# Head over seven gate/up pairs, two products for three, and gemvs moved to TensorE in a two-block transformer kernel

## The chip, the cores and the metric

The kernel runs on one core of one Trainium2 chip. The metric is the device time of one execution in microseconds. The engines are named as in the profile: PE is TensorE (PEld its weight loads), DVE VectorE, ACT ScalarE, POOL GpSimd, SP the engine that issues most DMAs.

## The reference, cut

Two blocks run on x of 256 rows and 1024 channels. The first has two layers; each is an FFN, a mixer (a pooling mixer, then attention) and a second FFN, and each of the three is modulated by vectors that come from c:

```python
mods = jnp.split(c_silu @ ada_w[layer] + ada_b[layer], N_MOD, axis=-1)
sh, sc, g = mods[0], mods[1], mods[2]
h = modulate(rms_norm(x, norm_g[layer, 0]), sh, sc)
x = x + 0.5 * (1.0 + g)[:, None, :] * swiglu(h, ffn_w_in[layer, 0], ffn_w_out[layer, 0])
```

`swiglu(h, w_in, w_out)` is `(silu(h @ w_g) * (h @ w_u)) @ w_out` with 2816 inner channels. The pooling mixer subtracts h from its mean over 2, 4, 8 or 16 rows, in four groups of channels, multiplies each group by a matrix, and scales. After the first layer keys and values are projected. The second block has a state-space branch and a latent attention, gated and merged. All is float32.

## The kernel before

x lies transposed as `X`: 128 channels on the partitions, eight slices kb, 256 rows of x in the free dimension. Every float32 weight tile of 512 KB (`wraw`, eight blocks of 128x128) is split into two float32r tiles: ACT casts it to the high part `whi` (L225), DVE subtracts to get the low part `wlo` (L216). The activations are split in the same way into `hhi` and `hlo`, in the FFN's inner layer into `shi` and `slo`. One block of a matrix product is then three products on PE, high by high, low by high, high by low (`mm3`, L350 to L352), each of 256 columns, into one PSUM bank. `mm3b` (L356 to L358) does the same with the roles exchanged and 512 columns.

The class `Stream` hands out weight tiles. Its `next()` splits tiles ahead of their use, up to four, and issues DMAs of later ones, with five raw buffers and five split ones. `Kernel.next` flushes functions that were put off (`defer`) by so many calls, and runs work from a list in the background by a budget. That list holds gemvs: `gemv(j)` takes a 512 KB tile of modulation weights (`graw`, three buffers) and the broadcast vector `cb` and writes 128 modulation values into column j of `modc`, in one DVE instruction (L377). A few gemvs run on PE instead, three at each seam between stages (`GAPS`, `gemv_pe`, L396), on tiles that were laid out for it. `ADA_SEQ` is the order of all gemv tiles in memory and on the DMA queue.

The order of all instructions is that of the code. Each engine works off its own queue in order, and so does SP with its DMAs; semaphores join them.

The FFN (`ffn`, L549) multiplies the input by pairs of gate and up tiles, 22 pairs; `act` applies silu on ACT (L558), multiplies on DVE (L560), copies the high part on ACT (L562) and subtracts on DVE (L563). The output tiles, eight of 22 blocks each, are added to X by `update` (L545), and ACT squares each new slice for the next norm (`st_add`), whose sums POOL adds up (L470) and PE reduces (`st_sum`, L486). `st_reduce` raises the sum to the power -1/2 on POOL (L506), `st_spread` turns it into a row by a transpose (L512). At a seam the parts of a PE gemv (`self.gap`) are issued between these steps.

The first FFN begins differently, since its modulation isn't there yet. This is the head: `ffn` works with four pairs at once (`lead`), slice by slice, and before slice k calls `feed(k)`, which takes the two gemvs of this slice (shift and scale, on DVE), modulates slice k of X (`mod_a`, L519 on DVE and L520 on ACT; `mod_b`, L524 on DVE) and splits one weight tile. PE then does the 4 x 2 x 3 products of the slice. The first norm's squares are added up by DVE and POOL.

In the pool stage (`pool_mixer`, L619) PE multiplies the modulated input by the group matrices; the result `pz` is multiplied by constant pooling matrices `pm`, an output tile at a time (L646, L647), and `update` follows.

## Time and profile before

| | us |
|---|---|
| median of three runs | 1333.29 (1330.23 to 1335.79) |
| the profiled execution | 1332.45 |
| its span, first to last instruction | 1330.6 |
| PE busy | 1274.8, 96% of the span, 10378 instructions |
| PE weight loads busy | 1210.3, 91% |
| DVE busy | 1008.7, 76%, 1751 instructions |
| ACT busy | 668.9, 50% |
| POOL busy | 163.9, 12% |
| DMA | 331.21 MB, mean 249 GB/s |

PE is busy nearly all the time, but its instructions overlap: one product is on record for 0.28 us, and the next starts 0.12 us after it. Its busy time therefore says that something was in it, not that it ran at its best, and spacings are what to read. The engines' shares are averages over stages that differ; the windows in the section of rows take the stages apart.

### The profile page before, as it was taken

The page shows a single profiled execution, that of the slowest core. Times are in us where ns is not written, and L with a number is a line of the kernel's source. Part 1 is how long each engine was busy: PE and PEld are TensorE (multiplying, and loading weights), DVE is VectorE, ACT ScalarE, POOL GpSimd, SP SyncE. Part 2 cuts the span into 40 slices and gives each one's busy share as a digit, 9 for nine tenths or more (in the row PEclk, how much of TensorE's full clock was granted, in tenths as well). Part 3 has the DMA queues.
Part 4 walks back from the last instruction along what each step waited for, and adds up shares of the span by engine and source line. Part 5 has one row for each costly group of instructions (what it writes and reads, how often), then busy time and mean ns, then how long its engine had stood idle before and what let it go on. Part 6 is the DMA issues. An engine that isn't in the chain of part 4 may idle for free.

```text
span 1330.6 us, 26407 instructions
## 1 busy us (share of the span) xinstructions
PE 1274.8 (96%) x10378; PEld 1210.3 (91%) x10378; DVE 1008.7 (76%) x1751; ACT 668.9 (50%) x1162; POOL 163.9 (12%) x282
## 2 busy tenths in 40 slices
PE   5899999999999999999998999999999999999998
PEld 4899999899999779999997989999988888988996
DVE  6898887698998789988977687878754576346774
ACT  3454434555444555444436554444365765236542
POOL 1000011100001100020111101000100791110000
PEclk9999999899999999999998999999999999989999
DMA  8999998487899578988974368877765533786752
GB/s 299 333 340 338 325 335 306 140 329 255 270 311 337 214 268 273 306 307 305 341 287 164 127 225 259 275 242 276 258 224 171 167 104 112 185 212 198 279 182 79
DMA packets 122287, 331.21 MB, mean 249 GB/s; under 512 B 27633, under 2 KB 42865, under 8 KB 122098
## 3 DMA queue, kind: packets, MB, share of 16 engines
q1 hardware_dynamic: 122018, 328.73, 72.9%
q8 instruction: 81, 1.33, 0.4%
q0 software_dynamic: 144, 0.79, 0.2%
q14 instruction: 44, 0.36, 0.1%
HBM read 317.94 MB, written 10.49 MB: 247 GB/s over the span
## 4 chain that ended last, share of the span: by engine, by line
PE 54%; ACT 4%; DVE 3%; DMA 3%; issue 1%; SPq 1%; POOL 0%; DVEq 0%; ACTq 0%; POOLq 0%
PE psA L350 5%; PE psA L352 4%; PE psB L352 4%; PE psB L350 4%; PE psB L351 4%; PE psA L351 4%; PE psD L350 3%; PE psD L352 3%; PE psD L351 3%; PE psC L350 2%; PE psC L352 2%; PE psC L351 2%; PE psA L356 1%; DMA wraw<-in_w 1%; PE psA L357 1%
## 5 line engine op out<-in xcount | busy, mean ns | idle before, releaser
L216 DVE TENSOR_TENSOR wlo<-wraw,whi 128x1024 fp32r<-128x1024 f32 x391 | 478.8, 1230 | 46.6 <-ACT whi L225 45.9
L225 ACT CAST whi<-wraw 128x1024 fp32r<-128x1024 f32 x391 | 403.4, 1047 | 120.3 <-ACT whi L225 46.9
L377 DVE SCALAR_TENSOR_TENSOR junk<-graw,cb 128x1024 bf16<-128x1024 f32 x166 | 203.9, 1228 | 24.6 <-DMA graw<-in_ada 21.0
L350 PE MATMUL psD<-hhi,whi 128*128 128x256 f32 x560 | 160.3, 286 | 0.4 <-ACT hhi L520 0.4
L352 PE MATMUL psD<-hlo,whi 128*128 128x256 f32 x560 | 159.1, 284 | 0.0
L351 PE MATMUL psD<-hhi,wlo 128*128 128x256 f32 x560 | 159.1, 284 | 0.0
L350 PE MATMUL psA<-hhi,whi 128*128 128x256 f32 x480 | 138.6, 289 | 5.0 <-ACT whi L225 3.3
L351 PE MATMUL psA<-hhi,wlo 128*128 128x256 f32 x480 | 137.3, 286 | 5.9 <-DVE wlo L216 5.9
L350 PE MATMUL psB<-hhi,whi 128*128 128x256 f32 x488 | 138.9, 285 | 0.0
L352 PE MATMUL psB<-hlo,whi 128*128 128x256 f32 x488 | 138.6, 284 | 0.0
L351 PE MATMUL psB<-hhi,wlo 128*128 128x256 f32 x488 | 138.6, 284 | 0.0
L352 PE MATMUL psA<-hlo,whi 128*128 128x256 f32 x480 | 136.7, 285 | 0.0
L350 PEld LDWEIGHTS psD<-hhi,whi 128*128 128x128 f32 x560 | 108.1, 193 | 2.1 <-issue 1.4
L352 PEld LDWEIGHTS psD<-hlo,whi 128*128 128x128 f32 x560 | 108.1, 193 | 0.2 <-DVE hlo L524 0.2
L351 PEld LDWEIGHTS psD<-hhi,wlo 128*128 128x128 f32 x560 | 108.1, 193 | 0.0
L350 PEld LDWEIGHTS psA<-hhi,whi 128*128 128x128 f32 x480 | 92.5, 193 | 8.8 <-ACT whi L225 4.5
L351 PEld LDWEIGHTS psA<-hhi,wlo 128*128 128x128 f32 x480 | 92.7, 193 | 7.3 <-DVE wlo L216 7.3
L350 PE MATMUL psA<-shi,whi 128*128 128x256 f32 x352 | 99.2, 282 | 0.0
L352 PE MATMUL psA<-slo,whi 128*128 128x256 f32 x352 | 98.6, 280 | 0.0
L350 PE MATMUL psB<-shi,whi 128*128 128x256 f32 x352 | 98.5, 280 | 0.0
L352 PE MATMUL psB<-slo,whi 128*128 128x256 f32 x352 | 98.5, 280 | 0.0
L351 PE MATMUL psB<-shi,wlo 128*128 128x256 f32 x352 | 98.1, 279 | 0.0
(453 smaller groups left out, 3201.4 us busy)
## 6 DMA issues: line engine op xcount, KB each, us to landing
graw<-in_ada SPq DMA_DIRECT2D x184, 512.0 KB
wraw<-in_win SPq DMA_DIRECT2D x176, 512.0 KB
wraw<-in_w SPq DMA_DIRECT2D x93, 512.0 KB
wraw<-in_wout SPq DMA_DIRECT2D x88, 512.0 KB
wraw<-in_wkv SPq DMA_DIRECT2D x16, 512.0 KB
Hd<-ct SPq DMA_DIRECT2D x16, 256.0 KB
Gd<-gsb SPq DMA_DIRECT2D x16, 256.0 KB
wraw<-in_wq SPq DMA_DIRECT2D x8, 512.0 KB
```

The lines of the kernel that those rows point to most:

```text
L216: self.nc.vector.tensor_sub(lo, raw, hi.bitcast(F32))
L225: self.nc.scalar.copy(hi, raw)
L350: mm(out, hi[:, b], ah, start=first, stop=False)
L351: mm(out, lo[:, b], ah, start=False, stop=False)
L352: mm(out, hi[:, b], al, start=False, stop=last)
L356: mm(out, ah, whi, start=first, stop=False)
L357: mm(out, ah, wlo, start=False, stop=False)
L377: self.nc.vector.scalar_tensor_tensor(junk, self.gemv_tile(j), 1.0, self.cb, op0=OP.mult, op1=OP.mult, accum_out=self.modc[:, j:j + 1])
```

## The change

It has three parts.

**The head.** `LEAD` is 7: seven pairs are computed slice by slice, in seven banks that hold gate and up side by side. The squares of X are no longer added up: each of the eight slices is reduced by PE, all into one PSUM tile. Eleven of the modulation tiles get buffers of their own (`headp`). The gemvs of six shift tiles (2, 4, 6, 8, 10, 12) run on PE, two in the middle of slices 0, 2 and 4 (`hooks` 7), and their results are transposed and added to the shift at the slice's end (`hooks` 14). The activations of pairs 0 to 5 are called within the last slice.

**Two products for three.** High and low part of an activation lie side by side in one tile (`hhl`, `shl`, `ohl`). In seven of eight output tiles of each FFN and of the attention's output projection, `mm2` multiplies the high weight by both parts at once, 512 columns, and the low weight by the high part, 256 columns. The bank then holds two sums, and `update` adds both to X.

**Gemvs in the pool stage.** The gap of the first FFN now holds tiles 54 to 56; tiles 57 to 63 are loaded into buffers of the pool stage and worked off on PE in two groups, ahead of its output tiles 0 and 4.

```diff
-HEAD_LAG = 1
+LEAD = 7
-    return 4 if (l, f) == (0, 0) else 2
+    return LEAD if (l, f) == (0, 0) else 2
-GAPS = {"g00": (61, 62, 63), "gpool": (64, 65, 66), "g01": (104, 105, 106), "g10": (128, 129, 130),
+GAPS = {"g00": (54, 55, 56), "gpool": (64, 65, 66), "g01": (104, 105, 106), "g10": (128, 129, 130),
-HEAD_PE = ()
+HEAD_PE = {0: (2, 4), 2: (6, 8), 4: (10, 12)}
+POOL_PE = ((57, 58, 59, 60), (61, 62, 63))
...
+    def mm2(self, out, hi, lo, b, a, first, last):
+        mm = self.nc.tensor.matmul
+        mm(out, hi[:, b], a.rearrange("p x t -> p (x t)"), start=first, stop=False)
+        mm(out[:, :T], lo[:, b], a[:, 0], start=False, stop=last)
...
     def update(self, kb, ps, g, eng=None, late=None):
-        self.nc.vector.scalar_tensor_tensor(self.X[:, kb], ps, g[:, kb:kb + 1], self.X[:, kb],
-                                            op0=OP.mult, op1=OP.add)
+        for i in range(0, ps.shape[1], T):
+            self.nc.vector.scalar_tensor_tensor(self.X[:, kb], ps[:, i:i + T], g[:, kb:kb + 1], self.X[:, kb],
+                                                op0=OP.mult, op1=OP.add)
...
+    def lead_pass(self, pp, hh, k, b, hooks):
+        for i, p in enumerate(pp):
+            for x in range(2):
+                if b % 8 == 0:
+                    self.lead_w = self.next()
+                hi, lo = self.lead_w
+                self.mm3(p[:, x * T:(x + 1) * T], hi, lo, b % 8, hh[:, k], k == 0 and x == 0, k == 7, True)
+                b += 1
+                if 2 * i + x + 1 in hooks:
+                    hooks[2 * i + x + 1]()
+        return b
...
+                pp = [self.ps(t) for t in "ABDDABC"]
...
+                self.lead_pass(pp, hh, KB - 1, b, {2 * i + 2: (lambda i=i: act(i - 1, pp[i - 1][:, :T], pp[i - 1][:, T:]))
+                                                   for i in range(1, n0)})
+                self.defer(act, n0 - 1, pp[-1][:, :T], pp[-1][:, T:])
...
-                    self.mm3(p[:, :T], hi, lo, b % 8, shi[:, k], slo[:, k], k == 0, k == FB - 1)
-                self.defer(self.update, n, p[:, :T], g)
+                    mm(p[:, :w], hi, lo, b % 8, ss[:, k], k == 0, k == FB - 1)
+                self.defer(self.update, n, p[:, :w], g)
...
+            for r in POOL_PE:
+                ts = [pp.tile([128, D], F32, name="pg%d" % j) for j in r]
+                for j, t in zip(r, ts):
+                    nc.sync.dma_start(t, self.h["ada"][ADA_POS[j]])
...
+                if n in (0, 4):
+                    side = self.gemv_pe(*gs[n // 4])
+                    side[0](0, KB)
+                    side[1](False)
+                elif n in (2, 6):
+                    side[2]()
...
+            for half in range(2):
+                for kb in (0, 2, 1, 3):
+                    kb += 4 * half
+                    sq = self.KT[:, kb]
+                    if kb % 4 < 2:
+                        nc.scalar.activation(sq, self.X[:, kb], AF.Square)
+                    else:
+                        V.tensor_mul(sq, self.X[:, kb], self.X[:, kb])
+                    if kb < 7:
+                        self.st_sum(sq, kb == 0, False)
...
+            self.st_reduce()
+            hgemv(1)
+            hgemv(0)
...
             def feed(k):
...
+                self.ws.split((14 * k + 21) // 8, los)
...
+                hr = self.mod_a(rbs, g0, h0, k)
+                los.pop(0)()
+                self.mod_b(hr, g0, h0, k)
+                while los:
+                    los.pop(0)()
+                js, n = more[k]
+                hdma(*js)
+                self.ws.dma(n)
                 if k + 1 < KB:
+                    hgemv(2 * k + 3)
...
+                def mm():
+                    pe[0](0, KB)
+                    pe[1](False)
+
+                def fin():
+                    nc.tensor.transpose(hps[:, 256:384], self.grow, self.ident)
+                    V.tensor_add(g0[:, 1, k + 1:k + 3], hps[:, 256:320:32], self.adab[:, js[0]:js[0] + 3:2])
+                    self.done.update(js)
+                return {7: mm, 14: fin}
```

How it moves instructions shows in the engines' queues; each row is line, operation, what it writes and reads, size, and the semaphores that it waits for by their engine. On DVE in the head, from one slice to the next, before (`junk` is a gemv, `hraw` and `hlo` are the modulation and the input's low part):

```order
L377 SCALAR_TENSOR_TENSOR junk,modc<-graw,cb 128x1024 [waits DMAHW5_49,DVE_49]
L998 SCALAR_TENSOR_TENSOR gain<-modc,gate 128x1
L1001 TENSOR_TENSOR gain<-modc,adab 128x1
L519 SCALAR_TENSOR_TENSOR hraw<-X,gain,rbs 128x256 [waits DVE_49]
L377 SCALAR_TENSOR_TENSOR junk,modc<-graw,cb 128x1024 [waits DMAHW6_49]
L524 SCALAR_TENSOR_TENSOR hlo<-hraw,gain,hhi 128x256 [waits Activation_49]
L216 TENSOR_TENSOR wlo<-wraw,whi 128x1024 [waits DMAHW4_49,Activation_49]
```

and after, from slice 0 to slice 1:

```order
L220 TENSOR_TENSOR wlo<-wraw,whi 128x1024 [waits DMAHW2_49]
L991 SCALAR_TENSOR_TENSOR junk,modc<-hg_149,cb 128x1024 [waits DMAHW5_49]
L1086 TENSOR_TENSOR gain<-psC,adab 128x2 [waits PE_49]
L1054 SCALAR_TENSOR_TENSOR gain<-modc,gate 128x1 [waits DVE_49]
L530 SCALAR_TENSOR_TENSOR hraw<-X,gain,rbs 128x256 [waits DVE_49]
L220 TENSOR_TENSOR wlo<-wraw,whi 128x1024 [waits DMAHW6_49,Activation_49]
L535 SCALAR_TENSOR_TENSOR hhl<-hraw,gain,hhl 128x256 [waits Activation_49]
```

One of two gemvs is gone, the low weight part stands ahead of the input's low part, and ahead of the modulation stands an add that waits for PE.

On ACT at the end of the head, from the last modulated slice on, before:

```order
L520 ACTIVATE hhi<-hraw,gain 128x256 [waits DVE_49]
L225 CAST whi<-wraw 128x1024 [waits DMAHW6_49,PE_49,Activation_49]
L225 CAST whi<-wraw 128x1024 [waits DMAHW0_49,PE_49,Activation_49]
L225 CAST whi<-wraw 128x1024 [waits DMAHW2_49,PE_49,Activation_49]
L225 CAST whi<-wraw 128x1024 [waits DMAHW3_49,PE_49,Activation_49]
L558 ACTIVATE sg<-psA 128x256 [waits PE_49]
L562 CAST shi<-sf 128x256 [waits DVE_49]
L225 CAST whi<-wraw 128x1024 [waits DMAHW4_49,Activation_49]
```

and after, the last of six activations and what follows it:

```order
L588 ACTIVATE sg<-psA 128x256 [waits PE_49,Activation_49]
L592 CAST shl<-sf 128x256 [waits DVE_49]
L588 ACTIVATE sg<-psB 128x256 [waits PE_49,Activation_49]
L592 CAST shl<-sf 128x256 [waits DVE_49]
L229 CAST whi<-wraw 128x1024 [waits DMAHW5_49]
L229 CAST whi<-wraw 128x1024 [waits DMAHW6_49]
```

Four more such pairs of a silu and a copy stand ahead of these, directly behind the modulated slice; no weight cast is among them.

On SP, from the end of the first FFN into the pool stage, before (`graw_2713` and the rows like it are gemv tiles in the three shared buffers):

```order
L211 DMA wraw_2681<-in_win01 128x1024 [waits DMAHW7_49,DMAHW0_49,DVE_49]
L363 DMA graw_2713<-in_ada 128x1024 [waits PE_49]
L363 DMA graw_2715<-in_ada 128x1024 [waits DMAHW1_49,PE_49]
L211 DMA wraw_2749<-in_win01 128x1024 [waits DMAHW3_49,DMAHW2_49,DVE_49]
L211 DMA wraw_2870<-in_win01 128x1024 [waits DMAHW4_49,DVE_49]
L363 DMA graw_2929<-in_ada 128x1024 [waits PE_49]
```

and after:

```order
L372 DMA graw_2575<-in_ada 128x1024 [waits PE_49]
L372 DMA graw_2577<-in_ada 128x1024 [waits DMAHW2_49,PE_49]
L215 DMA wraw_2611<-in_win01 128x1024 [waits DMAHW4_49,DMAHW3_49,DVE_49]
L661 DMA pg57_2663<-in_ada 128x1024
L661 DMA pg58_2664<-in_ada 128x1024 [waits DMAHW5_49]
L661 DMA pg59_2665<-in_ada 128x1024 [waits DMAHW6_49]
L661 DMA pg60_2666<-in_ada 128x1024 [waits DMAHW7_49]
L661 DMA pg61_2671<-in_ada 128x1024 [waits DMAHW0_49]
L661 DMA pg62_2672<-in_ada 128x1024 [waits DMAHW1_49]
L661 DMA pg63_2673<-in_ada 128x1024 [waits DMAHW2_49]
L215 DMA wraw_2745<-in_win01 128x1024 [waits DMAHW3_49,DVE_49]
L372 DMA graw_2873<-in_ada 128x1024 [waits DMAHW4_49,PE_49]
```

The seven loads of the pool stage stand behind two loads into shared buffers that wait for PE, and ahead of the tiles of the pool stage's own gap.

## Rows read from the trace of the kernel before

**Rows 1.** Windows: busy us (x instructions) of each engine, clock, DMA share, GB/s.

```profile
18.77:55.42 36.65, 29.66 (x192) 27.18 (x192) 31.99 (x63) 13.45 (x18) 0.00 (x0) 0.95 0.91 320
55.42:72.90 17.48, 17.48 (x145) 17.44 (x145) 16.83 (x28) 10.59 (x19) 0.00 (x0) 1.00 0.88 311
72.90:221.58 148.68, 148.68 (x1250) 148.55 (x1248) 125.20 (x178) 65.26 (x89) 7.86 (x7) 1.00 0.94 339
...
165.00:221.00 56.00, 56.00 (x478) 56.00 (x477) 44.94 (x58) 20.82 (x25) 7.86 (x7) 1.00 0.93 347
```

**Rows 2.** Timeline of PE, products of 512 columns: start us, us, what.

```profile
1301.32 0.40 PE L356 MATMUL psA<-whi,mh 128*128 128x512 f32 x1
...
1305.86 0.39 PE L358 MATMUL psB<-whi,ml 128*128 128x512 f32 x1
```

**Rows 3.** Timeline of PE in the head, with the idle time before an instruction.

```profile
11.80 1.01 PE L486 MATMUL psC<-ones,stacc 128*128 128x1 f32 x4 [5.79 <-POOL stacc L470]
12.67 0.99 PE L486 MATMUL psC<-ones,stlast 128*128 128x1 f32 x4
...
20.62 0.41 PE L350 MATMUL psB<-hhi,whi 128*128 128x256 f32 x1
20.84 0.41 PE L351 MATMUL psB<-hhi,wlo 128*128 128x256 f32 x1
...
34.81 0.58 PE L351 MATMUL psA<-hhi,wlo 128*128 128x256 f32 x1 [2.05 <-DVE wlo L216]
```

**Rows 4.** Timeline of ACT, start and end of the head.

```profile
5.00 0.42 ACT L459 ACTIVATE stacc<-X 128x256 f32<-128x256 f32 x1 [2.77 <-DMA X<-in_xT]
...
54.99 0.38 ACT L558 ACTIVATE sg<-psA 128x256 f32<-128x256 f32 x1
55.86 0.41 ACT L562 CAST shi<-sf 128x256 fp32r<-128x256 f32 x1 [0.49 <-DVE sf L560]
56.17 1.99 ACT L225 CAST whi<-wraw 128x1024 fp32r<-128x1024 f32 x2
```

**Rows 5.** Timeline of DVE, one slice of the head.

```profile
19.89 1.22 DVE L377 SCALAR_TENSOR_TENSOR junk<-graw,cb 128x1024 bf16<-128x1024 f32 x1
...
21.03 0.22 DVE L998 SCALAR_TENSOR_TENSOR gain<-modc,gate 128x1 f32<-128x1 f32 x1
...
21.28 0.48 DVE L519 SCALAR_TENSOR_TENSOR hraw<-X,gain,rbs 128x256 f32<-128x256 f32 x1
...
22.83 0.48 DVE L524 SCALAR_TENSOR_TENSOR hlo<-hraw,gain,hhi 128x256 fp32r<-128x256 f32 x1
23.28 1.23 DVE L216 TENSOR_TENSOR wlo<-wraw,whi 128x1024 fp32r<-128x1024 f32 x1
```

**Rows 6.** Timeline of PE, from the first FFN's end through the pool stage.

```profile
221.58 0.61 PE L396 MATMUL psC<-graw,cc 128*1 128x128 f32 x12
...
223.22 0.83 PE L396 MATMUL psC<-graw,cc 128*1 128x128 f32 x18
...
225.86 0.39 PE L356 MATMUL psA<-whi,hhi 128*128 128x256 f32 x1 [0.36 <-ACT hhi L520]
...
233.52 0.59 PE L646 MATMUL psA<-pm,pz 128*128 128x256 f32 x2
234.17 0.60 PE L646 MATMUL psB<-pm,pz 128*128 128x256 f32 x2
...
247.62 0.58 PE L350 MATMUL psA<-hhi,whi 128*128 128x256 f32 x1
```

**Rows 7.** Windows, with the granted clock (third from the end).

```profile
227.00:232.00 5.00, 4.67 (x34) 4.13 (x34) 4.68 (x11) 3.59 (x9) 0.00 (x0) 1.00 0.98 388
34.70:38.00 3.30, 3.19 (x15) 3.20 (x16) 3.30 (x9) 1.42 (x2) 0.00 (x0) 0.50 0.92 286
242.90:249.60 6.70, 6.13 (x52) 4.26 (x52) 4.31 (x9) 2.05 (x6) 1.62 (x1) 0.50 0.10 16
```

**Rows 8.** Timeline of SP's queue at the seam.

```profile
225.52 0.81 SPq L363 DMA_DIRECT2D graw<-in_ada  x2
```

More of the change, by code (lines that the diff above doesn't have):

```diff
@@ L80 @@
     ADA_SEQ += [j for j in range(a0, a1) if j not in ON_PE] + list(GAPS.get(gap, ()))
+    if gap == "g00":
+        ADA_SEQ += [j for r in POOL_PE for j in r]
 ADA_POS = {j: i for i, j in enumerate(ADA_SEQ)}
@@ L241, in next @@
         self.nh += 1
-        if self.nh >= 6 and self.ahead < HLB - 1:
+        if self.ramp and self.ahead < HLB - 1:
             self.ahead += 1
-            self.depth = RAWB
         return r
@@ L345, in flush, with mm3, mm @@
             f(*a)
-    def mm3(self, out, hi, lo, b, ah, al, first, last):
+    def mm3(self, out, hi, lo, b, a, first, last, shared=False):
+        def mm(*a, **kw):
+            self.nc.tensor.matmul(*a, skip_group_check=shared, **kw)
+        mm(out, hi[:, b], a[:, 0], start=first, stop=False)
+        mm(out, lo[:, b], a[:, 0], start=False, stop=False)
+        mm(out, hi[:, b], a[:, 1], start=False, stop=last)
+    def mm2(self, out, hi, lo, b, a, first, last):
         mm = self.nc.tensor.matmul
-        mm(out, hi[:, b], ah, start=first, stop=False)
-        mm(out, lo[:, b], ah, start=False, stop=False)
-        mm(out, hi[:, b], al, start=False, stop=last)
+        mm(out, hi[:, b], a.rearrange("p x t -> p (x t)"), start=first, stop=False)
+        mm(out[:, :T], lo[:, b], a[:, 0], start=False, stop=last)
     def mm3b(self, out, ah, al, whi, wlo, first, last):
@@ L604, in ffn, with proj_a @@
             self.st_half(D, gap)
-    def proj_a(self, ah, al, evac, kb=KB, tiles=8, tags="AB", T_=T, late=True):
+    def proj_a(self, a, evac, kb=KB, tiles=8, tags="AB", late=True, wide=0):
         hi = lo = None
@@ L934, in phase1, with hdma, hgemv @@
             ssm = self.ssm_items()
[L935 to L960 removed]
+            hs = ExitStack()
+            headp = hs.enter_context(self.tc.tile_pool(name="headp", bufs=1))
+            order = [2, 4, 3, 5, 6, 8, 7, 9, 10, 12, 11]
+            def hdma(*js):
+                for j in js:
+                    if j in order:
+                        t = headp.tile([128, D], F32, name="hg%d" % j)
+                    else:
+                        t = self.gpool.tile([128, D], F32, name="graw")
+                    nc.sync.dma_start(t, h["ada"][j])
+                    self.graw[j] = t
+            def hgemv(j):
+                junk = self.jpool.tile([128, D], BF, name="junk")
+                nc.vector.scalar_tensor_tensor(junk, self.graw.pop(j), 1.0, self.cb, op0=OP.mult, op1=OP.mult,
+                                               accum_out=self.modc[:, j:j + 1])
+                self.done.add(j)
+                self.slot()
+            hdma(1, 0)
+            self.cols = load("cols", [128, 100])
+            self.adab = load("adab", [128, NADA])
+            self.ws.dma(2)
+            hdma(2, 4, 3)
+            self.ws.dma(4)
+            hdma(5)
+            self.ws.dma(5)
             nc.scalar.activation(self.halfpi, self.ones, AF.Silu)
@@ L992, in phase1 @@
             V.tensor_mul(hg[:, 1], hg[:, 1], hg[:, 0])
+            more = [((6, 8, 7), 7), ((9,), 9), ((10, 12, 11), 11), ((13,), 12), ((14, 15), 14), ((), 16),
+                    ((), 18), ((), 19)]
             def feed(k):
@@ L1617, in zs_step @@
                     gelu(n - 6)
-            self.proj_a(hh, hl, zs_step, tags="CD", late=True)
+            self.proj_a(hh, zs_step, tags="CD", late=True)
             def gs_evac(n, p):
```

298 lines of the change are left out of this document (136 added, 162 removed).

## The prediction, made before the change was run

> **What bounds the kernel now.** I read the page's slices first, then windows by stage, then the queues at the places that the change touches. The windows [rows 1] show three kinds of stretch. From 72.90 to 221.58 us, the rest of the first FFN, PE is busy for all 148.68 us, one product every 0.12 us; the other three FFNs look the same. There only fewer or cheaper products help. From 18.77 to 55.42, the head, PE issues 192 products in 36.65 us, where 192 x 0.12 = 23 would do: it waits for DVE, which is busy for 31.99 us. The third kind is the seams between stages, of which the pool stage is one (221.6 to 247.6). So an edit is worth what it does to PE's products, to the head, and to that seam; DVE work removed from 72.90 to 221.58 is worth nothing.
>
> The profiled execution took 1332.45 us, with a span of 1330.6; the median of the three runs is 1333.29. The sum is made against 1332.45 and the difference of 0.8 is left within the range.
>
> **Edit 1: two products instead of three (output matmuls of the FFNs, 7 of 8 tiles, and 7 of 8 of the attention's).** It concerns 4 x 7 x 22 + 7 x 8 = 672 triples. Now each is three products of 256 columns; 478 of them stand in 56.00 us [rows 1], 0.118 us each with the edge rows off, 354 ns a triple. After, it is one of 512 and one of 256 columns. Products of 512 columns stand in the last stage: 20 spacings between 1301.32 and 1305.86, 227 ns each [rows 2]. So a pair costs 227 + 118 = 345, and 9 ns a triple are saved: what goes is the fixed part of one product, 2 x 120 - 227 = 13 ns at most. 672 x 9 = 6.3 us off PE's path; bounds 7 and 14 ns, so 4.5 to 9.5. The price is a second X update on DVE for 35 tiles, 0.39 us each. From 165 to 221 us, in the first output stage, DVE is busy for 44.9 of 56 us [rows 1], and 7 x 0.39 = 2.7 fits into the idle 11; without that cover all 35 would cost 14 us. I cost it at nothing.
>
> A page of the Trainium skill speaks against this edit: "TensorE: Matmul & The Clock Gate", section "Wait — 56ns, not 53.3ns?", gives a fixed cost of about 2.5 ns per matmul beside its columns. By it, as an estimate, 672 x 2.5 = 1.7 us would be saved. The spacings of 120 and 227 ns in this trace do not agree with it, and the sum goes by them.
>
> **Edit 2: the head.** Before, the 336th product ends at 72.9 us: 192 by 55.42 and 144 more in 17.48 [rows 1]. Those are 14 weight tiles' worth. After, the same 336 are seven pairs over eight slices, 42 products a slice. I work out when PE has done them.
>
> Start. The 16 sums of squares (two per slice of X) cost PE 0.87 us per slice at the early rate, from 11.80 to 12.67 [rows 3]. X is there at 5.0 [rows 4], so they end between 9 (at the full rate) and 12.4; I take 11.4. In DVE's new order the sums' result stands ahead of both first gemvs, so behind it come two gemvs of 1.14, gains, a modulation, a weight remainder of 1.14 and 0.45 for the input's remainder [rows 5], some 5 us, and further waits of about 1 us for ACT, whose two casts (1 us each) now stand ahead of the modulated input. PE starts in effect at 17.5 (16 to 18.5); before, its fourth product starts at 20.62 [rows 3], in effect 20.3.
>
> Products: 336 x 0.12 = 40.3. The first products before follow each other every 0.21 us [rows 3], and so for about 4.5 us; after such a start again, 2.6 us lost (1.7 to 3.4).
>
> Three gemv pairs in PE's queue, in the middle of slices 0, 2 and 4: three k-steps take 0.83 us [rows 6], whose last 0.27 overlap, so eight take 1.75; with the change of form 1.9 each, 5.7 together (5.2 to 6.6).
>
> **The new wait.** Behind slices 0, 2 and 4 PE transposes the gemv's row, DVE adds it to the shift, and only then come the gain and the modulation of the next slice, since DVE works in order. Queued behind that add are modulation, weight remainder and input remainder, for which PE waits. From [rows 4, 5]: transpose 0.3, add 0.15, gain 0.2, modulation 0.4 (start to start), weight remainder 1.14, input remainder 0.48. That is 2.7 until PE's third product; 0.24 of it is covered by two products that need no remainder. So 2.45 each, 7.4 for three (5 to 8). The odd slices need no such add: there DVE has 4.6 us of work from one input remainder to the next, PE 5.04, so DVE is hidden (0.2 for slice 7).
>
> The end of the head. Before, one activation stood ahead of each weight cast. Now ACT has six in a row, and each is silu, wait for DVE's product, copy: from 54.99 to 56.17 that takes 1.18 us [rows 4], while PE delivers a pair every 0.72. The first can start 36 products before PE's last, less 0.2 of latency, so 4.1 us. 6 x 1.18 = 7.1, so the next weight cast starts 2.9 us after it, takes 1.05, and its remainder 1.23: PE goes on 5.2 us late (3 to 6). Such waits have a second price: before product 34.81 PE was idle for 2.05 us [rows 3], and from 34.7 to 38.0 the granted clock was 0.50; from 242.9 to 249.6 it was so again [rows 7]. I add 2.0 for the one here (0 to 3.4) and 1.5 for the three smaller waits together (0 to 5).
>
> Sum: 17.5 + 40.3 + 2.6 + 5.7 + 7.4 + 0.2 + 5.2 + 3.5 = 82.4, against 72.9: **9.5 us slower**. All low ends together give 71.2, so -1.7; all high ends +18.8. I keep +2 to +16. DMA does not decide: the head needs 34 tiles of 512 KB, and the queue gave 388 GB/s [rows 7], 1.35 us a tile, so the last lands by 50 us, 15 ahead of its use. The gemvs' own buffers thus buy nothing beyond what PE can use.
>
> **Edit 3: seven gemvs from DVE to PE in the pool stage.** Off DVE go 7 x 1.22 = 8.5 us in a stretch where PE never waits: 0. On PE come two groups of 1.9, and a transfer: the seven tiles are loaded in the pool stage. SP comes to them at about 226, because two loads into the three shared buffers stand ahead (of tiles 57 and 58 a second time, which nothing reads) and wait until PE has read the gap's gemv (225.52, [rows 8]). Before the fourth of them then lie the pool matrix (768 KB, on POOL's queue), two tiles, a weight tile: 8.5 tiles x 1.31 to 1.35 from 226.4 is 237.9. PE is ready at 233.52 [rows 6]. So it waits 4.4 us; its clock, after that, falls as above. From there: group 1.75, four output tiles 2.6, group 1.75, four tiles 2.6 makes 246.7, with half the clock over part of it (+3.1) 249.8. From the last product of that loop to the next stage's first one it is 4.3 us at the other seam (221.58 to 225.86, [rows 6]): 254.1. Before it is 247.62, and at half the clock until 249.7, which makes 248.6 in effect [rows 6, 7]. Cost **+5.5, with the second gap's loads behind the seven +6** (3.5 without a drop of the clock, 10 with one that lasts into the next stage).
>
> The new layout (high and low part in one tile) moves nothing: same instructions, same sizes.
>
> **The sum.** 9.5 + 6 - 6.3 = +9.2: 1332.45 + 9.2 = **1341.7, said as 1342**. Half a per cent, 6.7 us, is about what a measurement of this kernel can tell from no change; the bounds are 1326.6 and 1340.
>
> **The rivals.**
> A, the clock stays at its upper level: statistics keep PE at work from 5 us on, and the waits of 2 to 5 us fall otherwise. Then 2.6 + 3.5 + 3 us go, and it gives 1333. For it: only one drop in the head before, with waits up to 2 us. Against: the low level after each of the longer waits in the trace.
> B, not slower: PE is not ahead of DVE at the slices' ends, because the add finds its transpose done, and the six activations run while PE still works on the last slice. The place is the head alone, the price 7.4 + 5.2 + 3.5 us; the sum becomes -7 and the time 1325.5. It decides as soon as more than 2.5 us of this go, for then the time is below 1340. Against: the add's operand is made behind the last product of the slice, and ACT's 1.18 per pair is longer than PE's 0.72.
> C, the clock falls in every one of the three slice waits and at both seams: +8, 1350.
> D, a product of 512 columns costs as much in the output stages as two of 256, 0.236 [rows 1]: edit 1 saves nothing, and it gives 1348. Against: the 227 ns a product [rows 2]. By the section of the Trainium skill cited under edit 1 it would come out near here.
> That the change doesn't do what it says has its place in B's opposite: statistics in PSUM end no earlier when PE works them off at the early rate. That is in the forecast.
>
> **How the numbers follow.** Forecast 0.50, A 0.22, B 0.15, C 0.08, D 0.05. The forecast's own spread (1334 to 1350) puts 0.14 of its 0.50 within half a per cent. So slower 0.36 + 0.08 + 0.05 = 0.49; within 0.14 + 0.19 of A + 0.05 of B = 0.38; faster 0.10 of B and 0.03 of A = 0.13. The range takes in B's time at its low end and C and the forecast's upper bounds: 1325 to 1353.
>
> **What would show it.** In the profile after: PE products of 512 and 256 columns 345 ns apart per pair in the output stages; the first product at 16 to 18.5 us; three waits of DVE's two-column add for PE, each followed by about 2 us of idle PE; six silu-copy pairs on ACT ahead of a weight cast near 75 us, and PE idle for 4 to 5 us there; product 336 at about 82; PE waiting for DMA at the pool stage's first gemv group; the pool stage some 32 us long instead of 26. Wrong if product 336 ends before 73, or if the group finds its tiles there.

## The result, and the profile after

The changed kernel takes 1356.82 us (median of 4 runs, 1351.56 to 1357.66), the kernel before 1333.64 in the runs beside it: a ratio of 1.0172, 95% interval 1.0151 to 1.0193. It is slower, by 23 us. The prediction said slower by 8.7, and 1353 at most. The profiled execution has a span of 1354.9 us against 1330.6, so there are 24.3 us to be found; one of the four runs, 1351.56, lies within the range of the prediction.

PE's timeline says where. "Product n" counts the gate/up products of the first FFN, and the seams are named by the first gemv of their gap on PE; all times are starts, in us.

| point on PE | before | after | lag | gained or lost there |
|---|---|---|---|---|
| product 1 | 18.77 | 18.41 | -0.4 | |
| product 336 (end of the head) | 72.78 | 78.38 | +5.6 | +6.0, the slices |
| product 400 | 80.46 | 93.73 | +13.3 | +7.7, the head's end |
| product 1056 (last gate/up) | 159.18 | 172.45 | +13.3 | 0 |
| seam behind the first FFN | 221.58 | 233.76 | +12.2 | -1.1, output tiles |
| seam behind the pool stage | 239.77 | 263.34 | +23.6 | +11.4, pool stage |
| seam behind the second FFN | 439.63 | 462.10 | +22.5 | -1.1 |
| seam behind keys, values, third FFN | 690.10 | 713.56 | +23.5 | +1.0 |
| seam behind the attention | 765.53 | 789.46 | +23.9 | +0.5 |
| seam behind the last FFN | 969.84 | 994.45 | +24.6 | +0.7 |
| end | 1330.6 | 1354.9 | +24.3 | -0.3 |

Head and pool stage hold it all. The windows of the changed kernel that answer to [rows 1] and [rows 7]; columns as there, busy us (x instructions) of PE, PEld, DVE, ACT, POOL, then granted clock, DMA share, GB/s:

```profile
18.41:78.50 60.09, 54.30 (x435) 50.45 (x435) 34.38 (x61) 19.19 (x32) 0.00 (x0) 0.94 0.68 251
32.00:36.00 4.00, 4.00 (x25) 4.00 (x25) 3.93 (x8) 0.51 (x1) 0.00 (x0) 0.68 0.80 273
84.00:90.00 6.00, 6.00 (x31) 6.00 (x32) 6.00 (x10) 4.04 (x5) 0.00 (x0) 0.57 0.73 260
178.00:233.00 55.00, 55.00 (x339) 49.56 (x338) 47.30 (x64) 20.77 (x25) 7.32 (x7) 1.00 0.95 344
250.00:256.00 6.00, 5.20 (x63) 3.16 (x64) 0.00 (x0) 0.88 (x4) 0.00 (x0) 0.50 1.03 414
```

DVE, which set the head's pace before, is busy for 34 of 60 us now. It waits for PE; the view of DVE's waits over the head (waited for: us in total, times, longest) has one large row:

```profile
DVE gain L1086 <- PE psC L1085: 22.5, 3, 8.1
```

That is the add of the transposed gemv row, and here is what it makes PE wait, at the first of the three places (PE's timeline from slice 0 to slice 1, idle time and releaser in brackets):

```profile
28.13 0.28 PE L353 MATMUL psC<-hhl,whi 128*128 128x256 f32 x1
28.25 0.27 PE L1085 MATMUL psC<-k_ident,grow 128*128 128x128 f32 x1
29.96 0.39 PE L353 MATMUL psA<-hhl,whi 128*128 128x256 f32 x1 [1.44 <-ACT hhl L531]
30.18 0.28 PE L353 MATMUL psA<-hhl,wlo 128*128 128x256 f32 x1
30.95 0.40 PE L353 MATMUL psA<-hhl,whi 128*128 128x256 f32 x1 [0.48 <-DVE hhl L535]
```

At 46 and 62 us the same two waits stand again. Then the end of the head, first on PE, then on ACT, where the last silu and copy stand ahead of the weight cast:

```profile
78.38 0.28 PE L353 MATMUL psC<-hhl,whi 128*128 128x256 f32 x1
82.59 0.58 PE L353 MATMUL psA<-hhl,whi 128*128 128x256 f32 x1 [3.93 <-ACT whi L229]
83.85 0.58 PE L353 MATMUL psA<-hhl,wlo 128*128 128x256 f32 x1 [0.68 <-DVE wlo L220]
```

```profile
80.32 0.38 ACT L588 ACTIVATE sg<-psB 128x256 f32<-128x256 f32 x1
81.18 0.41 ACT L592 CAST shl<-sf 128x256 fp32r<-128x256 f32 x1 [0.48 <-DVE sf L590]
81.50 1.99 ACT L229 CAST whi<-wraw 128x1024 fp32r<-128x1024 f32 x2
```

And the pool stage, where the first group of gemvs meets its tiles one by one as they land, and does its other 58 products at half the clock:

```profile
245.60 0.28 PE L367 MATMUL psB<-whi,hhl 128*128 128x256 f32 x1
247.64 0.38 PE L406 MATMUL psC<-pg,cc 128*1 128x128 f32 x2 [1.76 <-DMA pg<-in_ada]
248.82 0.38 PE L406 MATMUL psC<-pg,cc 128*1 128x128 f32 x2 [0.81 <-DMA pg<-in_ada]
250.10 0.58 PE L406 MATMUL psC<-pg,cc 128*1 128x128 f32 x2 [0.90 <-DMA pg<-in_ada]
251.38 3.57 PE L406 MATMUL psC<-pg,cc 128*1 128x128 f32 x58 [0.70 <-DMA pg<-in_ada]
254.89 0.80 PE L694 MATMUL psA<-pm,pz 128*128 128x256 f32 x1
```

So every wait that the prediction named is there. What it had too small are the prices, and the experiments take them apart. Total times of one kernel scatter by 2 to 9 us from run to run, so each experiment is read by its own stretch of PE's timeline first. Each of these stretches comes from one profile.

### The profile page after: what moved, and what is told of

The parts are those of the page before. It is cut to its first block, busy times and chain, and to the rows that moved or that the text cites. A ratio compares the mean times of both kernels' runs of the same rounds, so it can differ in the third digit from the quotient of the medians.

```text
span 1354.9 us, 25522 instructions
## 1 busy us (share of the span) xinstructions
PE 1295.1 (96%) x9943; PEld 1198.8 (88%) x9943; DVE 1012.3 (75%) x1759; ACT 670.1 (49%) x1171; POOL 158.4 (12%) x281
## 4 chain that ended last, share of the span: by engine, by line
PE 66%; DVE 12%; DMA 9%; ACT 5%; issue 5%; SPq 2%; POOL 1%; DVEq 0%; ACTq 0%; POOLq 0%
PE psD L353 14%; PE psB L353 14%; PE psA L353 13%; PE psC L353 5%; DVE wlo L220 4%; DMA graw<-in_ada 3%; PE psA L360 2%; DVE junk L386 2%; PE psB L360 2%; PE psA L361 1%; ACT whi L229 1%; DMA Ts<-Rd 1%; PE psC L406 1%; PE psB L361 1%; PE psA L365 1%
## 5 line engine op out<-in xcount | busy, mean ns | idle before, releaser
L353 PE MATMUL psA<-hhl,whi 128*128 128x256 f32 x960 | 254.9, 289 | 13.9 <-ACT hhl L531 8.5
L353 PE MATMUL psB<-hhl,whi 128*128 128x256 f32 x976 | 254.7, 286 | 0.0
L353 PE MATMUL psD<-hhl,whi 128*128 128x256 f32 x1120 | 221.8, 289 | 0.4 <-ACT hhl L531 0.4
L353 PEld LDWEIGHTS psA<-hhl,whi 128*128 128x128 f32 x960 | 185.7, 195 | 18.8 <-ACT hhl L531 10.8
L353 PEld LDWEIGHTS psB<-hhl,whi 128*128 128x128 f32 x976 | 188.4, 195 | 0.0
L353 PEld LDWEIGHTS psD<-hhl,whi 128*128 128x128 f32 x1120 | 185.0, 196 | 3.0 <-issue 2.1
L353 PE MATMUL psD<-hhl,wlo 128*128 128x256 f32 x560 | 160.9, 287 | 0.0
L353 PE MATMUL psB<-hhl,wlo 128*128 128x256 f32 x488 | 139.6, 286 | 0.0
L353 PE MATMUL psA<-hhl,wlo 128*128 128x256 f32 x480 | 137.4, 286 | 0.7 <-DVE wlo L220 0.7
L360 PE MATMUL psA<-shl,whi 128*128 128x512 f32 x352 | 123.9, 393 | 0.0
```

What stands on the lines that cost most here:

```text
L353: self.nc.tensor.matmul(*a, skip_group_check=shared, **kw)
L360: mm(out, hi[:, b], a.rearrange("p x t -> p (x t)"), start=first, stop=False)
```

## Experiments on the head

**All gemvs back on DVE** (`e_nohead`):

```diff
-HEAD_PE = {0: (2, 4), 2: (6, 8), 4: (10, 12)}
+HEAD_PE = {}
...
                     hgemv(2 * k + 3)
+                    hgemv(2 * k + 2)
...
```

> The changed kernel with all sixteen of the head's gemvs on DVE: no gemv on PE inside slices 0, 2 and 4, no transposes, no two-column add that waits for them. Theory: these cost the head three waits of 2.45, three gemv pairs of 1.9 to 2.5 and some 3.2 of low clock behind the waits, 16.5 in all; against it DVE has 5.8 us a slice (two gemvs 2.44, weight remainders 2.1, modulation 1.3) where PE has 5.04, 0.8 x 7 = 5.4 back. So 11 us less: product 336 starts near 67 instead of 78.4, time 1346 (1342 to 1350). Rival: DVE is then the bound as it was before the change, with more products behind each of its steps, and its 1.22 us gemvs cost what PE's waits did: 1354 or more.

Measured: 1341.43 (1340.24 to 1342.95), 15 us less than the changed kernel. Product 336 starts at 62.75, 15.6 earlier, and 10 earlier than before the change. The window of its slices 1 to 6:

```profile
25.00:57.00 32.00, 31.32 (x257) 30.71 (x256) 31.79 (x58) 11.66 (x15) 0.00 (x0) 1.00 0.85 316
```

DVE is busy for 31.79 of 32 us and PE for 31.32, at the full clock: with seven pairs a slice holds as much work for PE as for DVE. My estimate of 5.8 us of DVE work a slice took the instructions' durations; their spacings (1.14 for a gemv or a weight remainder) make 5.2, and PE has 5.04. So the mechanism holds and the gain was larger than expected, by 4 us. The rival, DVE as the bound, is nearly met, but costs 0.2 us a slice (5.28 against 5.04). Moving gemvs to PE took work off an engine that was no longer ahead of it.

**Work for PE in the three waits** (`e_fill`, `e_fill2`). Both put twelve products that nothing reads behind the transpose; in the first they stand ahead of the add in the program, in the second behind it. The edit of the second:

```diff
-                    nc.tensor.transpose(hps[:, 256:384], self.grow, self.ident)
-                    V.tensor_add(g0[:, 1, k + 1:k + 3], hps[:, 256:320:32], ...)
+                    nc.tensor.transpose(hps[:, 128:256], self.grow, self.ident)
+                    V.tensor_add(g0[:, 1, k + 1:k + 3], hps[:, 128:192:32], ...)
+                    for _ in range(12):
+                        nc.tensor.matmul(hps[:, 256:512], self.lead_w[0][:, 0], h0[:, k, 0], start=True, stop=True)
```

> The changed kernel with twelve products more behind each of the three transposes of the head; they write to a part of a bank that nothing reads, and keep PE at work for 1.44 us of each wait of 2.45. Theory: the low clock behind these waits comes from PE's idle time, so it stays away: granted clock 1.00 from 28 to 60 us, product 336 starts at 75 to 75.5 instead of 78.4, total 1353.5 (1350 to 1355.5). Rival: the clock falls in any case, for the granted clock also fell in some runs behind one wait and not behind another of the same length, or the products delay the next slice: product 336 at 78 or later.

> The changed kernel with twelve products more behind each of the head's three adds of the transposed row; they write to a part of a bank that nothing reads, and since they stand behind the add in the program, the add need not wait for them. Theory: PE is at work for 1.44 us of each wait, the wait itself (1.8 and 0.8 us) stays as long, and the low clock behind it stays away: granted clock 1.00 from 28 to 60 us, product 336 at 75 to 75.8. Rival: the clock falls behind one or two of the three waits as in the changed kernel (product 336 there between 75.8 and 78.4 in five profiles), idle PE for under a microsecond being enough or not the reason at all: product 336 at 77.5 or later. The total says less than this, 1350 to 1357.

The first, 1357.83 (1354.31 to 1361.35), is no test of its theory: the add waited for the twelve products too, since they write to the same tile, and the wait behind them stayed whole. Product 336 starts at 83.03, so the products delayed the slices, as the rival had it. PE's timeline:

```profile
27.31 1.67 PE L1087 MATMUL psC<-hhl,whi 128*128 128x256 f32 x12
30.49 0.39 PE L353 MATMUL psA<-hhl,whi 128*128 128x256 f32 x1 [1.51 <-ACT hhl L531]
...
31.48 0.39 PE L353 MATMUL psA<-hhl,whi 128*128 128x256 f32 x1 [0.49 <-DVE hhl L535]
```

The clock fell behind all three of these waits; slices 1, 3 and 5 last 7.38, 7.39 and 7.26 us. In the second the products lie in the wait:

```profile
28.05 1.70 PE L1088 MATMUL psC<-hhl,whi 128*128 128x256 f32 x12 [0.25 <-DVE gain L1086]
29.58 0.28 PE L353 MATMUL psA<-hhl,whi 128*128 128x256 f32 x1
...
30.23 0.50 PE L353 MATMUL psA<-hhl,whi 128*128 128x256 f32 x2 [0.24 <-DVE hhl L535]
```

and the windows behind the first and the second wait read

```profile
32.00:36.00 4.00, 4.00 (x36) 4.00 (x35) 3.93 (x8) 0.51 (x1) 0.00 (x0) 1.00 0.89 299
48.00:52.00 4.00, 4.00 (x36) 4.00 (x35) 2.57 (x4) 0.00 (x0) 0.00 (x0) 1.00 1.02 388
```

In the changed kernel the first of these windows stands at 0.68 (above). The second, and the one behind its third wait, read

```profile
48.00:52.00 4.00, 4.00 (x23) 4.00 (x23) 3.93 (x8) 0.51 (x1) 0.00 (x0) 0.57 0.94 369
62.00:68.00 6.00, 5.22 (x41) 5.02 (x42) 5.93 (x10) 3.58 (x5) 0.00 (x0) 1.00 0.63 171
```

Slices 1, 3 and 5 last 5.54 each, instead of 7.39, 7.37 and 5.88. The third of these, 5.88, is a slice at the full clock: the 0.34 between it and 5.54 has only moved, since slices 2 and 4 last 9.13 instead of 8.78 with the twelve products. So a fall of the clock costs 1.5 us (7.4 against 5.88), and the two of this execution 3.0. Product 336 starts at 74.65, just below the 75 to 75.8 expected and 3.7 earlier; the rest of the 3.7 is a quicker start in slice 0. In five other profiles of the same head product 336 lies between 75.7 and 78.2: the clock fell behind one of the three waits in four of them and behind two in the fifth. That it fell behind none where PE had work speaks for the idle time as the cause, but it is one profile, and the same waits without the work were often followed by 1.00 too. The total, 1346.3 in two runs, is lower than that explains; 3.3 us of the difference lie behind the last seam, where nothing was changed.

The Trainium skill ("TensorE: Matmul & The Clock Gate", section "What's actually happening") says that the lower clock is the default state and that activity releases it. These runs fit that: 1.00 behind all three waits where PE was given work, 0.50 in part of the windows behind two of the same waits without it.

**Activations spread** (`e_act`):

```diff
-                                                   for i in range(1, n0)})
-                self.defer(act, n0 - 1, pp[-1][:, :T], pp[-1][:, T:])
+                                                   for i in (1, 2)})
+                for i in range(2, n0):
+                    self.defer(act, i, pp[i][:, :T], pp[i][:, T:], lag=i - 1)
```

> The changed kernel with two of the head's seven silu-copy pairs inside the last slice and the other five put off, one per weight tile behind it, each behind that tile's weight cast on ACT. Theory: PE's 4.1 + 1.2 us between products 336 and 339, and the 2.1 us of low clock behind them, come from the six pairs ahead of the weight cast and go: 1349.5 (1348 to 1351.5). Rival: PE waits there for weight tiles in any case (SP's queue issues three tiles in 12 us from 73 on, buffers being short), and the wait only moves on by a tile or two: 1354 or more.

Measured: 1346.1 (1345.43 to 1347.8). The wait is gone:

```profile
78.20 0.28 PE L353 MATMUL psC<-hhl,whi 128*128 128x256 f32 x1
78.32 0.28 PE L353 MATMUL psA<-hhl,whi 128*128 128x256 f32 x1
78.92 0.38 PE L353 MATMUL psA<-hhl,wlo 128*128 128x256 f32 x1 [0.32 <-DVE wlo L220]
...
86.08 0.39 PE L353 MATMUL psD<-hhl,wlo 128*128 128x256 f32 x1 [1.15 <-DVE wlo L220]
```

A quarter of it has moved, as the rival had it, though not for its reason: a smaller wait for a weight remainder stands at 86. On DVE that remainder is queued behind a product that waits 1.50 us for ACT's silu (until 82.98) and behind a gemv; no weight tile is waited for. From product 336 to 400 it is 9.65 us, against 15.35 in the changed kernel and 7.68 before. Thus 5.7 of the 7.7 lost there are due to the order on ACT. The total fell by 10.7, to below the range expected; the other 5.0 are not shown to be due to the edit.

## Experiments on the pool stage

The stretch from the first seam's first gemv to the second's took 18.2 us before and 29.6 in the changed kernel. In five profiles of experiments that leave the pool stage as it is in the changed kernel it took 27.5 to 28.9; each gain below is to be read with that spread.

**Gemvs on a tile that is there** (`e_resident`):

```diff
-                    nc.sync.dma_start(t, self.h["ada"][ADA_POS[j]])
-                gs.append((r, ts))
+                gs.append(r)
...
-                    side = self.gemv_pe(*gs[n // 4])
+                    side = self.gemv_pe(gs[n // 4], [z[:, i % 2] for i in range(len(gs[n // 4]))])
```

> The changed kernel with the pool stage's two groups of gemvs working on a tile that lies in the chip already (the pool stage's own pz) instead of the loaded tiles 57 to 63, which are not loaded: these seven modulation values are wrong. PE's work is the same, only the loads are gone. Theory: of the 10.3 us in the pool stage 5.7 are the wait for four tiles, some 2 the low clock behind it, 3.5 the groups themselves; the first two go: 1349.5 (1348 to 1351.5). Rival: the groups on PE and the drop of the clock, which comes at this seam anyway, are the cost and the loads are hidden: 1354 or more.

Measured: 1344.55 (1341.62 to 1347.21); the stretch takes 21.6 us. PE goes from the last product (242.24) to the group and through it without a wait:

```profile
242.24 0.28 PE L367 MATMUL psB<-whi,hhl 128*128 128x256 f32 x1
242.45 1.93 PE L406 MATMUL psC<-pz,cc 128*1 128x128 f32 x64
244.31 0.70 PE L691 MATMUL psA<-pm,pz 128*128 128x256 f32 x2
```

So of the 11.4 us in this stretch 8.0 are the loads, with the drop of the clock that the wait for them brings, and 3.4 are the two groups as such (3.5 in the working ahead of the run). Against the 27.5 to 28.9 of the other profiles the loads are 5.9 to 7.3. The total, below the range expected, fell by more than the stretch explains.

**No second load of tiles 57 and 58** (`e_stale`):

```diff
-        if i < self.gend and i not in self.graw:
+        if i < self.gend and i not in self.graw and not 57 <= ADA_SEQ[i] <= 63:
```

> The changed kernel without the second loads of tiles 57 and 58 into the shared buffers, which nothing reads; the seven pool-stage tiles are then issued right behind the weight tile. Theory: the two loads are 2 x 1.3 us on the DMA queue ahead of the four tiles that PE waits for, so PE's wait of 5.7 us at the first group is 2 to 3 shorter: 1354 (1351 to 1356), with the stretch from the last group product to the end of the first group 3 us shorter. Rival: the queue is held by the buffers that the first FFN's end sets free, the tiles come as late as before: no change in that stretch.

Measured: 1348.24 in two runs; the stretch takes 27.0 us, 2.6 less. The first tile is there, the fourth still is not:

```profile
242.91 0.28 PE L367 MATMUL psB<-whi,hhl 128*128 128x256 f32 x1
243.17 0.38 PE L406 MATMUL psC<-pg,cc 128*1 128x128 f32 x2
...
246.91 3.51 PE L406 MATMUL psC<-pg,cc 128*1 128x128 f32 x58 [0.90 <-DMA pg<-in_ada]
```

PE waits until 246.91, 3.9 us instead of 5.7; in the five other profiles with both loads it waits 4.7 to 5.7. So the two loads are 0.8 to 1.8 us of the wait, where 2 to 3 were expected, and most of it is left. The total, 8.6 below the changed kernel and below its range, is not explained by this.

**No gemvs in the pool stage** (`e_nopool`):

```diff
-GAPS = {"g00": (54, 55, 56), ...
-POOL_PE = ((57, 58, 59, 60), (61, 62, 63))
+GAPS = {"g00": (61, 62, 63), ...
+POOL_PE = ()
...
```

> The changed kernel without its third part: tiles 57 to 63 go back to DVE in the first FFN's background and the gap holds 61 to 63. Theory (from the two traces: PE stands 12.2 us later at the first FFN's end and 22.5 later at the next FFN's first product, so the pool stage costs 10.3): the pool stage shrinks by 10.3, DVE's seven extra gemvs are hidden in the first FFN, 1346.5 (1344.5 to 1348.5). Rival: the seam costs this whatever stands in it, or DVE, which now also adds two sums to X, has no room for seven gemvs of 1.22 us and PE waits for weight remainders in the first FFN: 1353 or more.

Measured: 1348.34 (1344.07 to 1353.24). The stretch is back at 18.2. But the first output stage now takes 64.30 us (first to last product) instead of 60.98, and here the rival is right in part: PE waits for weight remainders. DVE and PE in it:

```profile
203.26 1.23 DVE L386 SCALAR_TENSOR_TENSOR junk<-graw,cb 128x1024 bf16<-128x1024 f32 x1 [2.15 <-DMA graw<-in_ada]
204.41 0.08 DVE L386 DVE_READ_ACCUMULATOR junk<-graw,cb 128x1 f32 x1
204.41 1.22 DVE L220 TENSOR_TENSOR wlo<-wraw,whi 128x1024 fp32r<-128x1024 f32 x1
```

```profile
205.68 0.38 PE L361 MATMUL psA<-shl,wlo 128*128 128x256 f32 x1 [1.74 <-DVE wlo L220]
```

A gemv on DVE waits 2.15 us for its tile, the weight remainder is queued behind it, and PE waits for that. DVE is busy for 56.9 of the stage's 64.3 us, and the DMA share is 0.95. I put the wait down to the background, which starts six weight tiles later than before, so that 18 gemvs fall on this stage instead of 15; that is argued and not shown, and `e_best3` below speaks against it. Taking seven gemvs out of the background was in any case worth 3.3 us in this kernel, where I had written 0.

## Experiments on the output products

**Three products again** (`e_mm3`; its edit follows), and **the kernel before with two products** (`e_mm2only`, which adds `mm2` and the second sum to the kernel before):

```diff
-                mm, w = (self.mm2, 2 * T) if n < KB - 1 else (self.mm3, T)
+                mm, w = self.mm3, T
...
-            self.proj_a(oo, lambda n, p: self.update(n, p, g), wide=KB - 1)
+            self.proj_a(oo, lambda n, p: self.update(n, p, g))
```

> The changed kernel with its second part undone: three products of 256 columns in all output tiles and one sum added to X; head and pool stage stay as changed. Theory: a pair took 346 to 347 ns in the changed kernel's first output stage (61.19 us against 62.28, 1.1 us less for 154 triples), so 672 pairs save 4.7 and without them the time is 1361 (1359.5 to 1363). Rival: the second X update on DVE and the wide products' longer hold of a PSUM bank cost elsewhere what they save (the four output stages together show only some 3 us, and small stalls of 0.5 to 1 us have appeared at later stages): 1357 or less.

> The kernel before with the second part of the change alone (two products for three in seven of eight output tiles of the FFNs and the attention); head, gaps and gemvs as before. Theory: with all 45 gemvs of the first FFN on DVE the second X update finds no cover there (in the run without gemvs in the pool stage the first output stage lasted 64.6 us instead of 61.2, PE waiting for weight remainders), so 4.7 saved less 3.4: 1332.5 (1330.5 to 1334.5), and PE waits of 1 to 2 us for weight remainders stand in the first output stage. Rival: the cover holds as the prediction had it, 1329 or less.

Measured: 1355.89 (1353.59 to 1357.04), 0.9 below the changed kernel; and 1331.08 in ten runs against 1332.73 of before, ratio 0.9987 (0.9966 to 1.0009). Neither differs from its partner by more than the scatter. The total of `e_mm3` is the one its rival named, but its head, in the same code, was 2.5 us quicker in the profile, so the total decides nothing. The stages themselves repeat to 0.1 us in most profiles, first to last product of each output stage:

| | 1st FFN | 2nd | 3rd | attention | 4th |
|---|---|---|---|---|---|
| before, and `e_mm3` | 62.07 | 63.97 | 62.89 | 22.99 | 65.57 |
| changed kernel | 60.98 | 63.38 | 62.99 | 22.46 | 64.74 |
| `e_mm2only` | 60.98 | 63.57 | 62.19 | 22.45 | 64.96 |

The edit saves 1.1 + 0.6 + 0.7 + 0.5 + 0.8 = 3.7 us (the changed kernel's third stage is 0.8 longer by a wait for a weight remainder that the other runs don't have). A pair takes 347 ns in the changed kernel's first output stage, where a triple took 353 to 354 before:

```profile
199.62 0.39 PE L360 MATMUL psB<-shl,whi 128*128 128x512 f32 x1
199.85 0.28 PE L361 MATMUL psB<-shl,wlo 128*128 128x256 f32 x1
199.97 0.39 PE L360 MATMUL psB<-shl,whi 128*128 128x512 f32 x1
```

In `e_mm2only` the second X update is hidden, as the prediction had it, and my later theory that it is not has fallen, though the total, 1331.08, lies in its range. With the earlier start of the background the same 45 gemvs made no long output stage, so it takes more than their number and the second update.

## Versions that keep what is good

`e_best1` takes the head of `e_nohead` and `e_act`, leaves the stale loads out and runs the pool stage's gemvs in three groups ahead of output tiles 2, 4 and 6. `e_best3` has that head and no pool gemvs, and spreads the background differently (`W_OUT` 0.9). `e_best4` adds one thing, the first two weight casts ahead of the copy of the norm's row:

```diff
             hgemv(0)
+            los0 = []
+            self.ws.split(2, los0)
             rb = self.st_spread()
...
```

> The changed kernel with three things undone or mended at once: all head gemvs on DVE, five of the seven head activations behind weight casts, and in the pool stage no second load of tiles 57 and 58, and three groups (two, two and three gemvs) ahead of output tiles 2, 4 and 6 instead of two ahead of 0 and 4. Theory: 15.4 and 7.3 to 10.7 as measured apart, and some 5 of the 10.3 in the pool stage: 1328 (1324 to 1333), below the kernel before. Rival: with the head 15 us shorter the weight tiles or DVE come late behind it, and the gains do not add up: 1336 or more.

> The changed kernel with all head gemvs on DVE, five of the seven head activations behind weight casts, no gemvs in the pool stage, and the weight that spreads the first FFN's background gemvs set to 0.9 instead of 1.2 per output tile, so that fewer of them fall on the output stage. Theory: the head as in the combined run before (product 400 at 72.4), the pool stage as before the change (18.2 us from seam to seam instead of 23.8), and the first output stage at 61.0, with no PE wait for weight remainders: 1323 (1319 to 1327). Rival: 45 gemvs don't fit beside the second X update and the later start of the background, as in the run without pool gemvs, where the first output stage took 64.3: 1327 or more.

> As the run before it, and the first two weight casts of the head stand on ACT ahead of the copy of the norm's row, in the time when ACT waits for the statistics, instead of between that copy and the modulated input. Theory: the first product comes up to 1 us earlier, at 17.4 instead of 18.4, total 1322 (1318 to 1326). Rival: the two weight tiles land only at about 15 to 16 us, the casts hold up the copy, and the first product is as late or later: 1323 to 1325.

Measured, ten runs each: 1328.37, ratio to before 0.9966 (0.9947 to 0.9985); 1326.82, 0.9965 (0.9948 to 0.9983); 1323.55, 0.9940 (0.9921 to 0.9959). All three are faster than the kernel before by under 1%, clear of the scatter, the last by 0.6%. In the last product 336 starts at 62.36, against 72.78 before, and product 400 at 72.0 (80.5 before). The first product starts at 17.52, 1.0 earlier, of which 0.4 are left at product 336; the rest of the 3.3 us between the last two is not shown to be due to this edit. Later groups in the pool stage (`e_best1`) find their tiles and leave a stretch of 23.8 us; without gemvs it is 18.2, but the first output stage then stays at 63.7 to 63.8 with 0.9 as well, so the theory that the weight of 0.9 cures it has failed. There 16 gemvs fall on the stage, as in the kernel before, where PE waits for nothing in it: why the stage is longer stays open.

## Why the prediction was wrong, step by step

The sign, the places and the kinds of wait were right. The steps that failed are sizes, of three terms: the seam behind the pool stage's loop (4.3 taken, 6.8 measured), the clock behind the slice waits (1.5 and 3.0), and the saving of two products for three (6.3 and 3.7). With the late end of slice 0 (1.2), the later fourth tile (1.3) and 3.8 us that no term had, the differences nearly all point the same way.

- **Start.** First product 16 to 18.5, in effect 17.5: it started at 18.41. The early rate held until about 24.4 and took most of the first gemv pair with it, so slice 0 ended 1.2 us later than worked out.
- **The new wait**, 2.45 each: 1.71 ahead of the slice and 0.84 in it (5.76 us in slice 5, at the full clock, for what takes 4.92 without a wait), 2.55. Right. Gemv pairs of 1.9 in slices 2 and 4: 1.91. Right.
- **The clock behind the three waits**, 1.5 together: 3.0 in this execution, 1.5 us longer slices twice. I took 0.5 for each wait, because the head before had many waits and one drop [rows 7], at the longest of them. In four of five other profiles of this head it fell once, which is the 1.5; so the term was right for most executions and too small for this one, and how often the clock falls is not in the code.
- **The end of the head**, 5.2 + 2.0: 7.7 from product 336 to 400. Right, and by the mechanism named. But "product 336 at about 82" doesn't follow from the working: that product stands ahead of this wait, at 82.4 - 7.2 = 75.2 by the sum, and ended at 78.5. The low and high ends add up to -1.5 and +18.5, not -1.7 and +18.8.
- **Edit 2 in all**: 13.3 instead of 9.5, within its own 2 to 16.
- **Edit 3**, 6, at most 10: it cost 10.9 until the second FFN's last gate/up product (lag 12.2 to 23.1), with the groups' 3.5 us in it. The wait for tile 60 was 5.7 instead of 4.4. The largest part of the error is the seam behind the loop: I took 4.3 from the other seam, and here it took 6.8 (263.34 to 270.10). Most of that is not the clock. This seam has a third sum, and PE waits twice for POOL in it; the other seam has one such wait, of 0.27 (236.49). After:

```profile
264.64 0.60 PE L497 MATMUL psC<-ones,stacc 128*128 128x1 f32 x4 [0.69 <-POOL stacc L481]
...
268.10 0.69 PE L523 MATMUL psC<-k_ident,strs 128*128 128x128 f32 x2 [1.13 <-POOL strs L517]
```

  In `e_nohead`, where the clock stood at 1.00 until 251.3, the same seam took 6.3 (245.73 to 252.03), with waits of 0.69 and 1.20:

```profile
250.49 0.43 PE L523 MATMUL psC<-k_ident,strs 128*128 128x128 f32 x2 [1.20 <-POOL strs L517]
```

  So 2.0 of the 2.5 us are the seam's own work and waits, and 0.5 the clock. A further 1.7, as an estimate, are the low clock on the next stage's first products (until about 273.5), which the sum had put into the time before (248.6 "in effect") and not into the time after. The pool stage, from its first gap to the next stage, was 36.3 us long and not 32. "Off DVE: 0" failed too: with the head's later background, seven gemvs more would have cost 3.3 us. That gain is in the changed kernel, but has no term of its own against the kernel before.
- **Edit 1**, 672 x 9 ns = 6.3, at least 4.5: it saved 3.7, 5.6 ns a triple, 7 in the first stage and 4 to 5.5 in the other FFNs. I compared spacings without edge rows (354 and 345); the pairs came to 347. By the 2.5 ns of the Trainium skill's section cited there, as an estimate, 1.7 us would be saved in all; the 3.7 measured are twice that, so it is too little as well.
- **What is left**: 13.3 + 10.9 - 3.7 = 20.5 of 24.3. The other 3.8 are a wait of 0.9 for a weight remainder in the keys and values, 1.0 in the attention, 0.8 in the third output stage, and 1.5 behind the attention's seam, where the clock fell; a gain of 0.3 stands against them. These differ from profile to profile in the same code, and I can't assign them to an edit.

Rival B, waits hidden in the head, fell: none was. Rival A fell with the clock, D with the output stages. Rival C comes nearest, with 1350 and a clock that falls more often; but the clock fell behind two of the three slice waits, in the wait of the pool stage and at the second seam, and stood at 1.00 through the first seam (232 to 238). The range failed by 4 us because several middling errors point the same way: the length of a seam was carried over from another seam that has other waits, and the drops of the clock entered as one small term, where they go with the waits that were forecast. In the six profiles of this head a drop that cost 1.5 us followed one or two of the three slice waits, and in every profile that has them a drop followed the longer waits at the head's end and in the pool stage.

## What to carry to other kernels

When a change makes one engine's steps longer (seven pairs a slice instead of four), work out anew which engine is ahead before moving work between them: here the longer slices alone had put PE level with DVE, and what was moved to PE then cost its own time, a round trip through ACT, PE and DVE, and the clock. A seam's time is to be read from that seam. A burst of small work on one in-order engine should leave room for the cast that the bottleneck needs next. An operand that is loaded for the gap in which it is used needs a gap that comes later than the loads that stand ahead of it.

## What the chip showed that I had not expected

- Idle times of 1.44 and 0.48 us, a few products apart, were followed by the lower clock, but not each time: behind the three equal waits of one execution the clock fell twice, in four other profiles once and in a fifth twice; with a little more idle time (1.51 and 0.49) three times, and with PE at work in one profile never.
- At the start of the products the clock can't be read from a window. The trace of the kernel before holds its first record of the clock at 24.4 us (the changed kernel's too); a window ahead of it reads 1.00 for want of a record, while products of 256 columns follow each other every 0.21 us, as at 0.50 later. From 24.45 on they are 0.12 apart. So records and spacings agree, and a 1.00 ahead of the first record says nothing.
- From the last gap's last product to the end, unchanged code took 353.1 to 360.0 us in the fourteen profiles, with the clock falling at different places. A single profile's total can't settle differences below some 5 us; the stages that repeat to 0.1 us can.
